# Reordering the end of a time-mixing kernel: an earlier unit's output between the last projections, and the last two slots evacuated and stored alone

## The chip, the cores and the metric

The kernel runs on one core of a Trainium2 chip. The metric is the device time of one execution in microseconds, as a median over several executions. The profile's span is shorter than that time by about 1.8 us.

## The reference

```
x_prev = x shifted by one step along the sequence, zero at the start
xv = x * time_mix_v + x_prev * (1 - time_mix_v)      # xk, k are not used by the output
xr = x * time_mix_r + x_prev * (1 - time_mix_r)
v  = xv @ value_weight;  r = xr @ receptance_weight
out = (sigmoid(r) * v) @ output_weight
```

The shapes are batch 16, sequence 2048 and width 256. Inputs and output are fp32.

## The kernel before

The work is cut into 64 units of 512 rows, four to a batch. A unit is transposed and mixed. Then come two projections (`r` and `v`, eight matmuls in all), a sigmoid on ScalarE, and a product on VectorE that gives `z`. One unit later, the output matmuls of `z` follow. The output of a unit goes from PSUM to `o_sb` by a ScalarE copy and from there to HBM by a store. Sequence rows are laid out so that a partition's row of `n` slots (a slot is 128 of the unit's rows) is one run of `n` KB in HBM.

```python
def store(queue, b, lo, hi):
    dst = out[b].rearrange("(p j) d -> p j d", p=P)
    queue.dma_start(out=dst[:, lo:hi, :], in_=o_sb[b][:, lo:hi, :])

def output(g, z):
    ...                                   # four slots of matmuls into ps (psum_o)
    nc.scalar.copy(out=o_sb[b][:, j0 : j0 + UJ, :], in_=ps)
    if b == B - 1:
        store(nc.sync, b, j0, j0 + UJ)
    elif e % 2 == 1:
        store(nc.sync, b, j0 - UJ, j0 + UJ)

def last_unit(g):                         # works by halves of 256 rows
    ...
    for h, (lo, hi) in enumerate(cols):
        project(banks[h], g, 0, lo, hi)
        nc.scalar.activation(out=s_sb[:, :, lo:hi], in_=banks[h], func=ACT.Sigmoid)
    for h, (lo, hi) in enumerate(cols):
        project(banks[2 + h], g, 1, lo, hi)
        nc.vector.tensor_tensor(out=z_sb[:, :, lo:hi], in0=s_sb[:, :, lo:hi],
                                in1=banks[2 + h], op=ALU.mult)
    ...
    for k, (pool, name) in enumerate(spare):      # k 0,1: unit before; k 2,3: this unit
        ...                                       # two slots of matmuls into ps
        if h == 0:
            nc.scalar.copy(out=o_sb[b][:, lo : lo + H, :], in_=ps)
        else:
            nc.vector.tensor_copy(out=o_sb[b][:, lo : lo + H, :], in_=ps)
        store(nc.scalar if k == 3 else nc.sync, b, lo, lo + H)
```

## Time and profile before

| what | value | read from |
|---|---|---|
| time | 213.88 us (213.71 to 214.05) | three executions |
| span | 212.8 us | the page; its execution took 214.59 us, longer than the three |
| first projection of the last unit starts | 203.70 us | the timeline |
| last copy ends | 207.43 + 0.69 = 208.12 us | the timeline |
| last store is issued / lands | 208.15 / 211.66 us | the timeline; 3.5 us to landing |
| **tail**: last unit's first projection to the end of the span | 212.83 - 203.70 = 9.13 us | worked out |

"At 3.83" in a tail means 3.83 us after the start of the last unit's first projection. The drain is the time in which the data of the stores flow out, and a landing is one of the sixteen completions that the records hold for each store. Instruction times are read from the timeline; first packets, instruction packets and landings are read from the packet and semaphore records of the same trace. Differences of such times can be off by 0.01. This is the part of it before the lines that the prediction shows. The columns are start, duration, engine, line, operation, output and inputs, shapes and count; a bracket tells the idle time before and what ended it.

```profile
203.70 0.60 PE L240 MATMUL psum_r<-mix,w_bf 128*128 128x256 bf16 x4
203.90 1.01 ACT L270 COPY o_sb<-psum_o 128x1024 f32<-128x1024 f32 x1 [0.66 <-PE psum_o L250]
...
204.93 3.25 SPq L260 DMA_DIRECT2D out_dram<-o_sb  x4
...
205.44 0.69 DVE L290 TENSOR_TENSOR z_sb<-s_sb,psum_v 128x512 bf16<-128x512 bf16 x1 [0.95 <-ACT s_sb L287]
```

ScalarE is in the copy of an earlier unit until 204.91, so its sigmoids, and with them VectorE's products, run late, and VectorE idles for 0.95 us. TensorE has work throughout, which the change uses.

### The profile page before, as it was taken

The page shows a single profiled execution, that of the slowest core. Times are in us where ns is not written, and L with a number is a line of the kernel's source. Part 1 is how long each engine was busy: PE and PEld are TensorE (multiplying, and loading weights), DVE is VectorE, ACT ScalarE, POOL GpSimd, SP SyncE. Part 2 cuts the span into 40 slices and gives each one's busy share as a digit, 9 for nine tenths or more (in the row PEclk, how much of TensorE's full clock was granted, in tenths as well). Part 3 has the DMA queues.
Part 4 walks back from the last instruction along what each step waited for, and adds up shares of the span by engine and source line. Part 5 has one row for each costly group of instructions (what it writes and reads, how often), then busy time and mean ns, then how long its engine had stood idle before and what let it go on. Part 6 is the DMA issues. An engine that isn't in the chain of part 4 may idle for free.

```text
span 212.8 us, 4177 instructions
## 1 busy us (share of the span) xinstructions
PE 202.0 (95%) x1566; PEld 134.9 (63%) x1593; DVE 193.8 (91%) x311; ACT 186.9 (88%) x202; POOL 77.1 (36%) x104
## 2 busy tenths in 40 slices
PE   8879999999999999999999999999999999999990
PEld 7537676666666666666666666666666666665570
DVE  1899999999999999999999999998999999999971
ACT  2688999998999999999999999999999999999870
POOL 1802331344453435434452444335343442344200
PEclk9999999999999999999999999999999999999998
DMA  5899999999969989998989999898989944443565
GB/s 181 196 176 216 240 288 285 326 234 337 245 152 288 277 228 339 176 348 179 291 243 225 340 200 354 157 325 211 260 283 216 354 200 197 197 172 162 208 249 200
DMA packets 9340, 51.91 MB, mean 244 GB/s; under 512 B 996, under 2 KB 1896, under 8 KB 3688
## 3 DMA queue, kind: packets, MB, share of 16 engines
q0 software_dynamic: 3008, 16.39, 43.9%
q1 hardware_dynamic: 6016, 34.87, 40.0%
q10 hardware_dynamic: 296, 0.40, 0.5%
q8 instruction: 12, 0.20, 0.3%
q14 instruction: 8, 0.07, 0.1%
HBM read 34.47 MB, written 33.55 MB: 320 GB/s over the span
## 4 chain that ended last, share of the span: by engine, by line
PE 73%; DVE 11%; DMA 5%; ACT 4%; issue 4%; POOL 1%; ACTq 0%; DVEq 0%
PE psum_o L250 22%; PE psum_v L240 20%; PE psum_r L240 19%; PE ps_t L173 10%; DVE z_sb L432 4%; DVE mix L229 3%; DMA x_bf<-in_x_dram 3%; DVE mix L207 2%; ACT s_sb L411 2%; DMA x_last<-in_x_dram 2%; ACT xt L178 1%; ACT o_sb L270 1%; PE ps_t L240 0%; ACTq L98 0%; POOL wo_bf L118 0%
## 5 line engine op out<-in xcount | busy, mean ns | idle before, releaser
L217 POOL TENSOR_SCALAR mix<-xt,c_sb 128x1024 bf16<-128x1024 bf16 (+1 forms) x61 | 64.4, 1057 | 117.0 <-DVE mix L229 101.4
L229 DVE TENSOR_TENSOR mix<-mix,xt 128x1024 bf16<-128x1024 bf16 (+1 forms) x129 | 90.0, 700 | 3.0 <-DVE mix L207 0.5
L432 DVE TENSOR_TENSOR z_sb<-s_sb,psum_v 128x1024 bf16<-128x1024 bf16 x63 | 76.6, 1216 | 4.8 <-PE psum_v L240 2.6
L270 ACT COPY o_sb<-psum_o 128x1024 f32<-128x1024 f32 x62 | 62.9, 1015 | 13.6 <-PE psum_o L250 13.2
L240 PEld LDWEIGHTS <-w_bf 128*128 128x128 bf16 x520 | 48.2, 98 | 35.4 <-issue 1.9
L240 PE MATMUL psum_v<-mix,w_bf 128*128 128x512 bf16 (+1 forms) x241 | 63.9, 377 | 1.7 <-DVE z_sb L432 0.6
L411 ACT ACTIVATE s_sb<-psum_r 128x1024 bf16<-128x1024 f32 x63 | 65.1, 1033 | 0.1
L250 PE MATMUL psum_o<-wo_bf,z_sb 128*128 128x256 bf16 x500 | 64.9, 273 | 0.2
L240 PE MATMUL psum_r<-mix,w_bf 128*128 128x512 bf16 (+1 forms) x244 | 64.0, 377 | 0.5
L178 ACT COPY xt<-ps_t 128x1024 bf16<-128x1024 bf16 x62 | 63.0, 1024 | 0.9 <-PE ps_t L173 0.9
L250 PEld LDWEIGHTS <-z_sb 128*128 128x128 bf16 x512 | 50.0, 98 | 19.1
L173 PEld LDWEIGHTS <-x_bf 128*128 128x128 bf16 x496 | 32.4, 98 | 15.6 <-DMA x_bf<-in_x_dram 2.4
L173 PE MATMUL ps_t<-ident,x_bf 128*128 128x128 bf16 x496 | 37.2, 219 | 1.6 <-DMA x_bf<-in_x_dram 1.4
L207 DVE TENSOR_SCALAR mix<-xt,c_sb 128x1024 bf16<-128x1024 bf16 (+2 forms) x89 | 35.5, 423 | 0.2
L91 POOL DMA_DIRECT2D x_bf<-in_x_dram x19 | 10.9, 577 | 0.0
L129 PE MATMUL ps_t<-zeros 128*128 128x128 bf16 x46 | 4.6, 289 | 1.0 <-DVE zeros L79 1.0
L129 PEld LDWEIGHTS <-zeros 128*128 128x128 bf16 x46 | 4.3, 135 | 1.0 <-DVE zeros L79 1.0
L399 ACT ACTIVATE mix<-xt,c_sb 128x512 bf16<-128x512 bf16 (+1 forms) x4 | 3.6, 930 | 0.0
L147 DVE COPY tm<-psum_o 128x4 f32<-128x4 f32 x1 | 0.2, 161 | 3.5 <-PE psum_o L143 3.5
L325 DVE COPY xt<-xt 128x254 bf16<-128x254 bf16 x15 | 3.3, 218 | 0.0
L112 ACT ACT_TABLE_LOAD x1 | 1.3, 1283 | 2.0 <-issue 2.0
L193 ACT CAST xt<-psum_r 128x512 bf16<-128x512 f32 x1 | 0.6, 585 | 2.5 <-PE psum_r L187 2.5
(45 smaller groups left out, 22.5 us busy)
## 6 DMA issues: line engine op xcount, KB each, us to landing
out_dram<-o_sb SPq DMA_DIRECT2D x30, 1024.0 KB, 7.1
x_bf<-in_x_dram POOLq DMA_DIRECT2D x14, 1024.0 KB, 10.8
x_bf<-in_x_dram POOLq DMA_DIRECT2D x4, 256.0 KB, 7.2
out_dram<-o_sb SPq DMA_DIRECT2D x2, 512.0 KB, 2.6
out_dram<-o_sb SPq DMA_DIRECT2D x3, 256.0 KB, 2.1
x_unit<-in_x_dram SPq DMA_DIRECT2D x2, 256.0 KB, 3.9
x_unit<-in_x_dram SPq DMA_DIRECT2D x1, 512.0 KB, 5.6
x_bf<-in_x_dram POOLq DMA_DIRECT2D x1, 512.0 KB, 10.9
```

Of the source, the lines that this page charges most:

```text
L91: nc.gpsimd.dma_start(out=x_bf[b][:, lo:hi, :], in_=rows(b)[:, lo:hi, :])
L129: nc.tensor.matmul(out=ps, lhsT=zeros, rhs=zeros, start=True, stop=True)
L173: nc.tensor.transpose(out=ps[:, ko, jj * P : (jj + 1) * P], in_=src[:, jj, ko * P : (ko + 1) * P], identity=idn,)
L178: nc.scalar.copy(out=xt[b][:, :, c0 : c0 + TU], in_=ps)
L207: nc.vector.tensor_scalar(out=mix[b][:, m, ko, lo:hi], in0=xt[b][:, ko, lo:hi], scalar1=c_sb[:, m, ko : ko + 1], scalar2=None, op0=ALU.mult,)
L217: op = nc.gpsimd.tensor_scalar(out=mix[b][:, m, 1, lo:hi], in0=xt[b][:, 1, lo:hi], scalar1=c_sb[:, m, 1:2], scalar2=1.0, op0=ALU.mult, op1 ...
L229: return nc.vector.tensor_tensor(out=mix[b][:, m, :, lo:hi], in0=mix[b][:, m, :, lo:hi], in1=xt[b][:, :, lo + P : hi + P], op=ALU.add,)
L240: nc.tensor.matmul(out=ps[:, mo, :], lhsT=w_bf[:, m, ko, mo * P : (mo + 1) * P], rhs=mix[b][:, m, ko, e * TU + lo : e * TU + hi], start=(k ...
L250: nc.tensor.matmul(out=ps[:, slot, :], lhsT=z[:, ko, jj * P : (jj + 1) * P], rhs=wo_bf[:, ko, :], start=(ko == 0), stop=(ko == KO - 1),)
L270: nc.scalar.copy(out=o_sb[b][:, j0 : j0 + UJ, :], in_=ps)
L411: nc.scalar.activation(out=s_sb, in_=ps_r, func=ACT.Sigmoid)
L432: nc.vector.tensor_tensor(out=z_sb, in0=s_sb, in1=ps_v, op=ALU.mult)
```

## The change

The intent is to start the evacuation and the stores of the last unit but one earlier, and to make the very last evacuation and store small. The first half of that unit's output moves ahead of the last value projection, and the second half follows it. ScalarE evacuates both halves, and VectorE the last unit's first half. The last two slots each get a bank (the code's word for a PSUM tile that takes one result), a copy (one on ScalarE, one on VectorE) and a store of 128 KB (one from Scalar, one from Sync). The core of the diff:

```diff
+        def out_part(pool, name, z, unit, jj, n, copy, queue):
+            ps = pool.tile([P, n, D], FP32, name=name)
+            for k in range(n):
+                out_matmuls(ps, z, jj + k, k)
+            lo = unit * UJ + jj
+            copy(out=o_sb[b][:, lo : lo + n, :], in_=ps)
+            store(queue, b, lo, lo + n)
+
+        by_act, by_dve = nc.scalar.copy, nc.vector.tensor_copy
 ...
         for h, (lo, hi) in enumerate(cols):
             project(banks[2 + h], g, 1, lo, hi)
             nc.vector.tensor_tensor(...)
-        ... (the loop over k shown above)
+            pool, name = [(ps_o_pool, "psum_o"), (ps_r_pool, "psum_r")][h]
+            out_part(pool, name, z_prev, e - 1, h * H, H, by_act, nc.sync)
+        out_part(ps_v_pool, "psum_v", z_sb, e, 0, H, by_dve, nc.sync)
+        out_part(ps_t_pool, "ps_t", z_sb, e, H, 1, by_act, nc.scalar)
+        out_part(ps_t_pool, "ps_t", z_sb, e, H + 1, 1, by_dve, nc.sync)
```

More of the change, by code (lines that the diff above doesn't have):

```diff
@@ L292, in last_unit @@
             )
-        spare = [(ps_o_pool, "psum_o"), (ps_r_pool, "psum_r"), (ps_v_pool, "psum_v"), (ps_t_pool, "ps_t")]
-        for k, (pool, name) in enumerate(spare):
-            ps = pool.tile([P, H, D], FP32, name=name)
-            h = k % 2
-            for jj in range(H):
-                out_matmuls(ps, z_prev if k < 2 else z_sb, h * H + jj, jj)
-            lo = (e - 1) * UJ + k * H
-            if h == 0:
-                nc.scalar.copy(out=o_sb[b][:, lo : lo + H, :], in_=ps)
-            else:
-                nc.vector.tensor_copy(out=o_sb[b][:, lo : lo + H, :], in_=ps)
-            store(nc.scalar if k == 3 else nc.sync, b, lo, lo + H)
+            pool, name = [(ps_o_pool, "psum_o"), (ps_r_pool, "psum_r")][h]
[3 more added lines that the diff above has]
+        out_part(ps_t_pool, "ps_t", z_sb, e, H + 1, 1, by_dve, nc.sync)
     def tile_for(b):
```

## The prediction

> **What bounds the kernel now.** I read the page's busy shares first, then its chain of waits, then only the last ten microseconds, because the diff touches nothing earlier: the instruction orders of the two kernels are the same on every engine up to the last unit.
>
> ```profile
> PE 202.0 (95%) x1566; PEld 134.9 (63%) x1593; DVE 193.8 (91%) x311; ACT 186.9 (88%) x202; POOL 77.1 (36%) x104
> PE 73%; DVE 11%; DMA 5%; ACT 4%; issue 4%; POOL 1%; ACTq 0%; DVEq 0%
> ```
>
> The body is bound by TensorE (95% busy, 73% of the chain). The change keeps the number of matmuls and only reorders the last ones, so the body's time stays. What it can move is the end: evacuations and stores after the last projections. The timeline of the last unit (start, duration, engine, line, operation; bracket: idle time before):
>
> ```profile
> 204.80 0.60 ACT L287 ACTIVATE s_sb<-psum_r 128x512 bf16<-128x512 f32 x1
> 205.29 0.60 ACT L287 ACTIVATE s_sb<-ps_t 128x512 bf16<-128x512 f32 x1
> ...
> 206.05 0.68 DVE L290 TENSOR_TENSOR z_sb<-s_sb,ps_t 128x512 bf16<-128x512 bf16 x1
> 206.08 0.59 ACT L301 COPY o_sb<-psum_o 128x512 f32<-128x512 f32 x1 [0.18 <-PE psum_o L250]
> ...
> 206.64 0.68 DVE L303 COPY o_sb<-psum_r 128x512 f32<-128x512 f32 x1
> 206.78 0.61 PE L250 MATMUL ps_t<-wo_bf,z_sb 128*128 128x256 bf16 x4
> 206.95 0.59 ACT L301 COPY o_sb<-psum_v 128x512 f32<-128x512 f32 x1 [0.29 <-PE psum_v L250]
> 207.43 0.69 DVE L303 COPY o_sb<-ps_t 128x512 f32<-128x512 f32 x1
> 208.15 0.38 ACTq L260 DMA_DIRECT2D out_dram<-o_sb  x1
> ```
>
> Computing ends at 208.12, but the span at 212.8: 4.7 us are transfers and the closing barrier. What the closing wait is for, from the waits of the Sync queue after 206 us, and the DMA view from 207 to 211.4 us (40 slices of 0.11 us):
>
> ```profile
> SPq L468 <- DMA out_dram<-o_sb: 3.3, 4, 1.4
> DMA  2000288999999999999999989989981320010000
> q1 hardware_dynamic: 450, 0.79, 48.3%
> q10 hardware_dynamic: 144, 0.26, 16.2%
> q14 instruction: 2, 0.02, 1.3%
> out_dram<-o_sb SPq DMA_DIRECT2D x3, 256.0 KB, 2.1
> out_dram<-o_sb ACTq DMA_DIRECT2D x1, 256.0 KB, 3.5
> ```
>
> The reader should see three things. The DMA engines are idle from 207.1 to 207.5, then full until 210.3: four stores of 256 KB (1.05 MB) back to back, so the drain is bound by bytes, not by the last copy. The last store lands 3.5 us after its issue, at 208.15 + 3.5 = 211.65, against 2.1 us for the stores ahead of it, since it queues. And there is a thin tail after 210.3, in which queue 14 moves two 8 KB packets of instructions: in the packet records 15 of the 16 completion packets of the last store start by 210.44, and the last one at 211.18. From the last landing to the end are 212.83 - 211.66 = 1.17 us of further waits and barrier.
>
> [...]
>
> **The change part by part.** Four matmuls of 128x256 take 0.44 us in the chain (109 ns spacing).
>
> First, the output of the earlier unit's first half moves ahead of the last value projection. Its matmuls end at 205.61 instead of 206.04. They need the psum_o bank, which ScalarE's 128x1024 copy leaves at 204.91 (203.90 + 1.01); PE gets there at 205.01, so I expect no stall, or under 0.1 us. The copy does not gain the whole 0.44: ScalarE is in the second sigmoid until 205.89, and its successive halves start 0.49 apart, so the copy starts at 205.29 + 0.49 = 205.78 and ends at 206.37, against 206.67 before. Its store goes out 0.3 us earlier, at about 206.40.
>
> Second, the last value projection ends 0.44 later, at 206.04. VectorE could start that product no earlier than 206.05 before; now at about 206.08. It loses 0.03 us, and PE's first matmul on it goes from 206.78 to 206.81. This is the main reason why the reorder costs nothing.
>
> Third, the earlier unit's second half: PE still ends it at 206.48, but ScalarE takes it (206.52 to 207.11) instead of VectorE (206.64 to 207.32). Store 0.21 us earlier, at about 207.14.
>
> Fourth, the last unit's first half moves from ScalarE (206.95 to 207.54) to VectorE (206.96 to 207.64). Before, its store had to wait for Sync, which needs 0.33 us plus 0.13 between issues, until 207.81; now it goes at 207.67. Gain 0.14.
>
> Fifth, the last two slots. With slopes from this trace (ScalarE (1012 - 586)/512 = 0.83 ns an element, VectorE (1216 - 690)/512 = 1.03) a 256-wide copy is 0.37 us on ScalarE and 0.42 on VectorE. Slot one: PE done at about 207.19, copied by 207.60, store from Scalar at 207.63. Slot two: PE done at 207.42, VectorE free to start at 206.96 + 0.60 = 207.56, done at 207.98; but Sync is issuing until 208.00 and needs 0.13 more, so it issues at 208.13. Before, the last issue was at 208.15. **So the last issue does not move**; only the bytes behind it shrink from 256 to 128 KB.
>
> What counts is then the drain. First data follow an issue by 0.8 us (206.69 to 207.5). The first store's data can start at 206.40 + 0.8 = 207.2, just as the 512 KB store ahead ends, so the idle 0.3 us is filled. The second is ready at 207.14 + 0.8 = 207.95, the first needs until 207.9: a gap of 0.05. Later ones queue. The drain took 210.44 - 207.5 = 2.94 us. The last two stores now have 1 KB packets: 46 ns median (the 1 KB loads of this trace) against 84 for the 2 KB packets of the tail, 8 packets per engine and store, so 2 x 8 x (46 - 42) = 0.06 us more. New end: 207.2 + 2.94 + 0.05 + 0.06 = 210.25 instead of 210.44, a gain of 0.19. The closing wait takes completion semaphores in a fixed order at 0.065 us each: four came after the last store's before, now three. Sum: about 0.25 us off. To this I add a little for the chance below: **213.55 us**.
>
> **The rivals.** (a) The fetch tail. In this execution instruction packets held one engine's last completion from about 210.79 (the other landings) to 211.66: 0.87 us. If the moved instructions shift or split that fetch, up to 0.87 + 0.25 = 1.1 us goes, 212.8. For: it is only two packets, and Scalar reaches its end branch at 208.0 instead of 208.5. Against: whatever its moment, the fetch still adds its time to an engine that has a full queue. I give it one in six. (b) The Sync queue becomes the bound: five issues, and if Scalar's issue at 207.63 excludes Sync's at 207.67 (both issues near 208.15 show about 0.37 instead of 0.33), the last goes at about 208.45, its data at 209.25. The queue is still full until after 210, so nothing or 0.1 us is lost: 213.7 to 213.9. (c) The drain is limited by the last copy, as the intent supposes: the gain is then the last copy's, 208.12 to 207.98, some 0.14 us: 213.7. The full DMA slices speak against it. (d) PE stalls on psum_o and pushes everything: at most 0.1 us, against a slack of 0.1 in the records.
>
> **Range and chances.** The mechanism bounds the gain at the idle hole (0.3 to 0.4 us) unless the fetch tail goes too, and the kernel before itself spreads over 213.71 to 214.05. So 212.9 to 214.1. Two per cent is 4.3 us, nearly all of the 4.7 us after the last copy; neither side is plausible: 0.01 faster, 0.98 same, 0.01 slower.
>
> **What would show it.** Right: the earlier half's copy at about 205.8, stores issued near 206.4 and 207.1, no idle DMA slice between 207.1 and 207.5, the last issue still at 208.1 or later, last packets near 210.25. Wrong: if the drain is no longer full before the last store (then the last issue decides), if 1 KB packets take far more than 46 ns, or if the two instruction packets land elsewhere or not in the tail.

## The result, and the profile after

Two sets of rounds were run. Here and in all the experiments, a ratio is the mean time of one kernel's fast runs over that of the other's of the same rounds, so it is not quite the ratio of the medians quoted.

| | median, us | before, same rounds | ratio, 95% interval |
|---|---|---|---|
| after, first | 214.00 (213.70 to 214.58) | 213.86 | 1.0009 (0.9993 to 1.0025) |
| after, again | 213.70 (213.63 to 214.22) | 213.86 | 0.9997 (0.9981 to 1.0014) |

The times do not tell the two kernels apart. The page of the changed kernel shows the same body; the chain of waits is the third line:

```profile
span 212.4 us, 4180 instructions
PE 201.5 (95%) x1566; PEld 134.6 (63%) x1593; DVE 193.8 (91%) x311; ACT 187.1 (88%) x203; POOL 77.3 (36%) x104
PE 74%; DVE 10%; DMA 5%; issue 4%; ACT 2%; POOL 1%; ACTq 0%; DVEq 0%
```

The end of its timeline:

```profile
203.56 0.60 PE L240 MATMUL psum_r<-mix,w_bf 128*128 128x256 bf16 x4
...
204.87 0.60 PE L250 MATMUL psum_o<-wo_bf,z_sb 128*128 128x256 bf16 x4
...
205.31 0.60 PE L240 MATMUL ps_t<-mix,w_bf 128*128 128x256 bf16 x4
...
205.64 0.60 ACT L291 COPY o_sb<-psum_o 128x512 f32<-128x512 f32 x1
...
206.01 0.69 DVE L300 TENSOR_TENSOR z_sb<-s_sb,ps_t 128x512 bf16<-128x512 bf16 x1
...
206.38 0.59 ACT L291 COPY o_sb<-psum_r 128x512 f32<-128x512 f32 x1
206.76 0.33 PEld L250 LDWEIGHTS <-z_sb 128*128 128x128 bf16 x4 [0.26 <-DVE z_sb L300]
...
206.82 0.69 DVE L291 COPY o_sb<-psum_v 128x512 f32<-128x512 f32 x1
207.19 0.37 ACT L291 COPY o_sb<-ps_t 128x256 f32<-128x256 f32 x1 [0.22 <-PE ps_t L250]
207.43 0.41 DVE L291 COPY o_sb<-ps_t 128x256 f32<-128x256 f32 x1
207.59 0.38 ACTq L260 DMA_DIRECT2D out_dram<-o_sb  x1
```

The reader should see that the output matmuls at 204.87 stand between the value projections, that the copies of the earlier unit are early, and that the last copy ends at 207.84. Only one matmul group pays: the first matmul on the last unit's second half waits for VectorE (0.26 us idle on the weight side). The DMA view from 207 to 211.4 us and the closing wait of the Sync queue, as shown for the kernel before:

```profile
DMA  0898998889999999999998999994210100000000
...
q14 instruction: 2, 0.02, 0.9%
...
out_dram<-o_sb SPq DMA_DIRECT2D x1, 128.0 KB, 3.3
```

```profile
SPq L471 <- DMA out_dram<-o_sb: 2.3, 3, 1.5
```

The idle hole ahead of the drain is gone (0.1 us is left of 0.4). The two instruction packets are still there, and so is the thin tail behind the data. On the common clock of the tail, in microseconds (stores named by what they carry: first and second half of the earlier unit, first half of the last unit, last two slots):

| in the tail | before | after |
|---|---|---|
| stores issued | 2.99, 3.65, 4.11, 4.45 | 2.71, 3.43, 3.98, 4.03 and 4.42 |
| first data packet | 3.83 | 3.55 |
| 8 KB instruction packets start | 6.52, 6.75 | 6.32, 6.60 |
| last landing | 7.96 | 7.76 |
| end of span | 9.13 | 8.86 |

So the tail became 0.27 us shorter: 0.20 in the last landing and about 0.07 in the waits behind it. The repetition gave 8.84 for the same kernel. Why the times do not show it is seen at the other end. From the ninth unit's first projection to the last unit's, both kernels need 166.71 us (203.70 - 36.99 and 203.56 - 36.85), and the repetition needs 166.70. But the ninth unit starts at 36.99, 36.85 and 36.31 us in these three profiles. In these profiles the starts therefore scatter by 0.7 us, more than twice the tail's gain. The other executions have no profile, so that their times differ by the start is inferred. It is not shown that this gain of the tail reaches the whole time: the first interval, 0.9993 to 1.0025, leaves out the 0.9987 that the gain alone would give.

### The profile page after: what moved, and what is told of

Its sections match the earlier page's. It is cut to its first block, busy times and chain, and to the rows that moved or that the text cites. A ratio compares the mean times of both kernels' runs of the same rounds, so it can differ in the third digit from the quotient of the medians.

```text
span 212.4 us, 4180 instructions
## 1 busy us (share of the span) xinstructions
PE 201.5 (95%) x1566; PEld 134.6 (63%) x1593; DVE 193.8 (91%) x311; ACT 187.1 (88%) x203; POOL 77.3 (36%) x104
## 4 chain that ended last, share of the span: by engine, by line
PE 74%; DVE 10%; DMA 5%; issue 4%; ACT 2%; POOL 1%; ACTq 0%; DVEq 0%
PE psum_o L250 22%; PE psum_v L240 21%; PE psum_r L240 20%; PE ps_t L173 10%; DVE z_sb L435 4%; DVE mix L229 3%; DMA x_bf<-in_x_dram 3%; DVE mix L207 2%; ACT s_sb L414 2%; DMA x_last<-in_x_dram 2%; ACT xt L178 0%; PE ps_t L240 0%; ACTq L98 0%; POOL wo_bf L118 0%; DVE o_sb L291 0%
```

## The experiments

The first four kernels ran on one chip, the next four on a second and the last four on a third, each set beside its own runs of the kernel before.

**The changed kernel again.**

> The changed kernel unaltered, to settle its time. In the two profiles the tail, from the start of the last unit's first projection to the end of the span, fell from 212.83 - 203.70 = 9.13 us to 212.42 - 203.56 = 8.86. Theory (the store drain ends earlier and nothing else changes): ratio about 0.9987, that is 0.27 us less. Rival (something outside the tail costs what the tail gains, or the tail of one profile was luck): ratio 1.000 or above, as in the first measurement (1.0009). In the profile: last landing again about 7.8 us after the start of the last unit.

Measured: 213.70 us, ratio 0.9997 (0.9981 to 1.0014), tail 8.84, last landing at 7.76. The tail's gain is real and repeats to 0.02 us. The interval includes both 0.9987 and 1.000, so this time settles nothing by itself.

**The reorder alone.**

```diff
-            out_part(pool, name, z_prev, e - 1, h * H, H, by_act, nc.sync)
-        out_part(ps_v_pool, "psum_v", z_sb, e, 0, H, by_dve, nc.sync)
-        out_part(ps_t_pool, "ps_t", z_sb, e, H, 1, by_act, nc.scalar)
-        out_part(ps_t_pool, "ps_t", z_sb, e, H + 1, 1, by_dve, nc.sync)
+            out_part(pool, name, z_prev, e - 1, h * H, H, [by_act, by_dve][h], nc.sync)
+        out_part(ps_v_pool, "psum_v", z_sb, e, 0, H, by_act, nc.sync)
+        out_part(ps_t_pool, "ps_t", z_sb, e, H, H, by_dve, nc.scalar)
```

> The reorder alone: the earlier unit's first half before the last value projection, but the evacuations on the engines of before and the last two slots together. Theory (the drain is bound by the time at which data are there and then by bytes): the first store goes out 0.3 us earlier, but the second still waits for VectorE and goes when it went before, so the hole in the DMA moves from before the first store to behind it: tail 9.05 to 9.15 us, ratio 1.000. Rival (the first store's time alone decides): tail 8.85, ratio 0.9987.

Measured: 214.38 us, ratio 1.0025 (1.0006 to 1.0043), tail 9.31. The DMA view from 206.9 to 211 us (slices of 0.10 us) shows the hole at the place expected:

```profile
DMA  5999998100399998999999999999997110101000
```

The first store starts at 3.56 and is done by 4.3; then the engines idle until the second arrives. The tail is 0.16 us worse than my range allowed. Of the 0.18 us that it is longer than before, 0.11 is in the last landing and 0.07 in the closing waits, among which the last store had an earlier place. VectorE has to finish the last product first (to 3.14 us) before it can copy the second half, so the second store goes out at 3.77, later than the 3.65 of before, and so do all stores after it (4.23 and 4.57 against 4.11 and 4.45). An early first store was worth nothing with the others later.

**The other half alone.**

```diff
-            pool, name = [(ps_o_pool, "psum_o"), (ps_r_pool, "psum_r")][h]
-            out_part(pool, name, z_prev, e - 1, h * H, H, by_act, nc.sync)
+        out_part(ps_o_pool, "psum_o", z_prev, e - 1, 0, H, by_act, nc.sync)
+        out_part(ps_r_pool, "psum_r", z_prev, e - 1, H, H, by_act, nc.sync)
```

> The other half alone: matmuls in the order of before, ScalarE evacuates both halves of the earlier unit, VectorE the last unit's first half, the last two slots each alone. Theory (bytes from the first store on): the first store goes when it went before, the queue is then full to the end, so the drain ends 0.06 us later for the 1 KB packets, less 0.065 for one closing wait: tail 9.05 to 9.2 us, ratio 1.000. Rival (the last copy and the last store's size decide): tail 8.8 to 8.9, ratio 0.9987 or less.

Measured: 214.20 us, ratio 1.0016 (0.9996 to 1.0036), tail 9.20, first data at 3.83 as before. A small last store by itself gains nothing, although its last copy ends at 4.29 instead of 4.42. In both half versions two instruction packets are in the tail (last landings at 8.07 and 8.12), as in the kernel before; they were not run again without them.

**Moving VectorE's instruction packet.** The packets of queue 14 come at places that look like fixed counts of instructions: in the changed kernel VectorE had started 70, 193, 328 and 447 instructions at four of the eight, 119 to 135 apart. That these four are VectorE's was an estimate. The edit shifts VectorE's count by 24:

```diff
     warm_up(WARM)
+    pad = consts.tile([P, 1], FP32)
+    for _ in range(24):
+        nc.vector.memset(pad, 0.0)
```

> The changed kernel with 24 one-column memsets on VectorE in its idle time at the start. In the changed kernel's records 15 of the last store's 16 completions land by 210.79 and the last at 211.32, beside two 8 KB instruction packets at 209.88 and 210.16. Theory (one of these packets is VectorE's next block, fetched when it reaches a fixed count of instructions, as its earlier packets come about 128 instructions apart): with 24 more instructions one packet moves to about 195 to 200 us, and the last landing comes 0.3 to 0.8 us earlier: tail 8.1 to 8.6 us against 8.86. Rival (both packets are set off by the jump to the closing block, or by other engines): both stay in the tail, tail 8.8 to 8.9, and the time is equal or up to 1 us more if the memsets delay the start.

Measured: 214.12 us, ratio 0.9998 (0.9975 to 1.0020), tail 8.34, last landing at 7.25. The DMA view of this kernel from 206 to 211 us, with the last store's time to landing in its final column:

```profile
q14 instruction: 1, 0.01, 0.4%
...
out_dram<-o_sb SPq DMA_DIRECT2D x1, 128.0 KB, 2.8
```

The DMA view from 196 to 199 us:

```profile
q14 instruction: 1, 0.01, 0.6%
```

One packet left the tail and came at 197.5 us. At their packets VectorE had started 447 instructions without the memsets and 451 with them. The last store lands 2.8 us after its issue instead of 3.3. The tail is 0.5 us shorter than that of the changed kernel, but the time does not show it: two of the six executions took 213.1 us, the profiled one among them, and four 214.1 to 214.4. What distinguishes them the single trace can't say, and a cost of the memsets at the start of those four is not excluded here. The versions with the late stores below carry the same memsets, and their times fall by about what their tails do.

**Moving Sync's packet too, with the change and without it.**

```diff
+        elif e % 2 == 1 and b < 3:
+            store(nc.sync, b, j0 - UJ, j0)
+            store(nc.sync, b, j0, j0 + UJ)
         elif e % 2 == 1:
```

> The changed kernel with the 24 memsets on VectorE and, in the first three batches, each 1024 KB store of Sync as two of 512 KB (12 more Sync instructions). With the memsets alone one instruction packet left the tail (it came 5.6 us before the last unit) and the tail fell from 8.86 to 8.34 us; the other still came 6.64 us into it. Theory (that one is Sync's next block, as Sync reached its 80th instruction 1.0 to 1.4 us before it in both kernels): it moves to about 195 to 200 us, 3 to 8 us before the last unit, the last landing comes with the others, tail 8.15 to 8.3 us. Rival (it belongs to the jump to the closing block or to ScalarE): it stays at 6.6 us and the tail at 8.34. The median time should be 0.5 us or more under the changed kernel's on the same start; the starts of six profiles differ by up to 0.7 us, so the ratio may still be between 0.995 and 1.000.

> The kernel of before with the same memsets and the same split stores: the change's own effect without the instruction packets is then this run against e5_both_pads. Theory (the packets delay any last store that is under way): both leave the tail, which falls from 9.13 to 8.2 to 8.45 us, and the distance to e5 is the drain's gain of 0.2 plus 0.065 for a closing wait, or less if the packets cost before more. Rival (the packets do not touch the kernel before in this way): tail 9.0 to 9.2.

Measured: with the change 214.34 us, ratio 1.0016 (0.9987 to 1.0045), tail 8.24; without it 214.40, ratio 1.0005 (0.9977 to 1.0033), tail 8.34. In both, the second packet moved to 0.37 us before the last unit and no engine's completion is late any more (last landings at 7.02 and 7.07). Sync had started 82 instructions at its packet, both in the changed kernel and in the first of these. Both packets therefore go with instruction counts, one with VectorE's (447 and 451) and one with Sync's (82 and 82). They had delayed the last landing by 0.74 us after (7.76 - 7.02) and 0.89 before (7.96 - 7.07). The tails shrank by less, 0.62 and 0.79, because the edits also move the last store to an earlier place among the closing waits, which costs 0.09 to 0.12 us. Without the packets the change is worth only 0.10 us: 0.05 in the last landing and the rest in the closing waits.

The times missed, and the trace says why. Units 4 to 8 took 14.73 us in the first of the two and 14.21 in the second, against 13.49 before. The waits of the weight loads in those units of the first:

```profile
PEld L176 <- DMA x_bf<-in_x_dram: 1.3, 1, 1.3
```

A transpose waited 1.3 us for its input. With the memsets alone those units took 13.50 us. In the kernel before, the mean DMA share in these units is 1.01, and 0.93 in units 32 to 44.

**Is the drain bound by bytes or by the last copy?** Two looks, both on the version with both packets moved. The first leaves out one store (with None as its queue, `out_part` skips it; wrong rows), the second delays the last copy.

```diff
-        out_part(ps_v_pool, "psum_v", z_sb, e, 0, H, by_dve, nc.sync)
+        out_part(ps_v_pool, "psum_v", z_sb, e, 0, H, by_dve, None)
```

> e5_both_pads without the store of the last unit's first half (256 KB); those rows of the output are wrong on purpose. Copies and all other issues stay. Theory (the drain is bound by bytes, the last issue at 4.42 us having 0.6 us to spare): the last landing comes 0.5 to 0.7 us earlier than in e5. Rival (the last copy and its issue set the end): the last landing moves by less than 0.1 us.

```diff
+        slack = consts.tile([P, H, D], FP32)
+        nc.vector.tensor_copy(out=slack, in_=x_unit[:, 0, 0:H, :])
         out_part(ps_t_pool, "ps_t", z_sb, e, H + 1, 1, by_dve, nc.sync)
```

> e5_both_pads with an idle VectorE copy of 128x512 ahead of the last copy, which delays the last copy and its store by 0.3 to 0.5 us. Theory (the queue is still full when the last store comes): the last landing moves by less than 0.1 us. Rival (the last copy sets the end): it moves by the whole delay.

Measured: without 256 KB the last landing comes at 6.28 instead of 7.02, 0.74 us earlier. The delayed version's timeline:

```profile
208.07 0.42 DVE L314 COPY slack<-x_unit 128x512 f32<-128x512 f32 x1
208.24 0.38 ACTq L263 DMA_DIRECT2D out_dram<-o_sb  x1
208.40 0.42 DVE L297 COPY o_sb<-ps_t 128x256 f32<-128x256 f32 x1
```

Its last copy starts at 4.20 in the tail instead of 3.87, and the last issue goes from 4.40 to 4.64. The last landing goes from 7.02 to 7.05. So 0.24 us of delay of the last store costs 0.03, while a store of 256 KB costs 0.74: without the packets the drain is bound by what is stored and not by the last copy. Leaving out a store takes away bytes and a store at once; that the number of stores counts too is shown below.

**The split stores later.**

```diff
-        elif e % 2 == 1 and b < 3:
+        elif e % 2 == 1 and 8 <= b < 11:
```

> e5_both_pads with the split stores in batches 8 to 10 instead of 0 to 2. In e5 the four units from 4 to 8 took 14.73 us against 13.50 with the memsets alone, so the gain of the tail was lost there. Theory (the first units are short of DMA, so extra stores there delay the loads; later ones are free): units 4 to 8 take 13.5 us again, tail 8.24 as in e5, time 0.6 us under the changed kernel on the same start: ratio to before 0.995 to 0.998. Rival (split stores cost wherever they are): units 32 to 44 take over 0.3 us longer than 36.55 us.

> The kernel of before with the memsets and the late split stores. Theory: tail 8.34 us as in e6, so nearly all of the 0.9 us that can be had in this tail is the instruction packets', not the change's: ratio 0.995 to 0.998, within 0.001 of e9. Rival (the change is worth its 0.27 us of the two first profiles): tail 8.5 or more.

Measured beside 214.16 us for the kernel before: with the change 213.14, ratio 0.9956 (0.9943 to 0.9969), tail 8.25; without it 213.53, ratio 0.9972 (0.9955 to 0.9988), tail 8.34. Units 4 to 8 took 13.66 us in the first of these, and units 32 to 44 took 36.56: the splits cost nothing measurable there. The DMA views of the two drains, with the change (from 206.4 to 210.3 us, 0.10 us a slice) and without it (from 206.6 to 210.7):

```profile
DMA  8999995999998999999898999999940000000000
...
q1 hardware_dynamic: 570, 0.91, 62.6%
q10 hardware_dynamic: 144, 0.13, 9.7%
```

```profile
DMA  7000039899999999899999999999999850000000
...
q1 hardware_dynamic: 456, 0.82, 53.4%
q10 hardware_dynamic: 144, 0.26, 16.7%
```

Neither has a line for queue 14, and neither has a thin tail: where the data end, the row falls to 0 within two or three slices (9, 4, 0 and 9, 8, 5, 0). The changed kernel's row starts earlier without a hole and takes as long again at its end. The two ratios differ by 0.0016, but their intervals overlap, and only 0.09 us of it, 0.0004, is in the tails; the two profiled executions differ otherwise in the start of the ninth unit, at 36.11 and 36.64 us.

**One last store.**

```diff
-        out_part(ps_t_pool, "ps_t", z_sb, e, H, 1, by_act, nc.scalar)
-        out_part(ps_t_pool, "ps_t", z_sb, e, H + 1, 1, by_dve, nc.sync)
+        out_part(ps_t_pool, "ps_t", z_sb, e, H, 1, by_act, None)
+        out_part(ps_t_pool, "ps_t", z_sb, e, H + 1, 1, by_dve, None)
+        store(nc.sync, b, e * UJ + H, (e + 1) * UJ)
```

> e9_late_pads, but the last two slots, still copied apart by ScalarE and VectorE, leave in one store of 256 KB from Sync (2 KB packets, no store on Scalar's queue). In e5 the last 512 KB landed in 7.02 - 5.49 = 1.53 us, in e6 in 7.07 - 5.71 = 1.36. Theory (the two 128 KB stores with 1 KB packets on two queues cost 0.15 to 0.2 us of drain): the last landing comes at 6.8 to 6.9 us into the last unit, against 7.02. Rival (the store that waits for the last copy is what counts, and it is now twice as large): last landing 7.1 or later. The tail gets one closing wait of 0.06 us more for its place in their order: 8.05 to 8.2 us.

Measured: 213.24 us, ratio 0.9950 (0.9938 to 0.9962), last landing at 6.82 against 7.03 with two stores, tail 8.08. The store is issued at 4.41 in both. So storing the two slots apart, which is one of the two aims of the change, costs 0.21 us of landing. Of that, 0.09 is data (the last packet ends at 6.47 instead of 6.56) and the rest is the time from the last packet to the last landing (0.35 instead of 0.47). With two stores, the last one's sixteen completions begin at 6.82, as the Scalar store's last one has landed at 6.81, and take 0.21 us; with one store they take 0.12 (6.70 to 6.82). Whether they wait for each other, and how much is due to packet size, the number of stores or the second queue, is not shown. Against the kernel before without packets, whose last landing is at 7.06, the reorder with one last store gains 0.24, about the 0.27 by which its first data are earlier; the split gives nearly all of that back. These are differences of tails: the times with two stores and with one, 213.14 and 213.24, do not differ clearly.

**The last store's place among the closing waits.**

```diff
-        elif e % 2 == 1 and 8 <= b < 11:
+        elif e % 2 == 1 and 6 <= b < 12:
```

> e10_one_store with twelve split stores, batches 6 to 11, instead of six, so that the last store takes the last of the eight completion semaphores that the closing waits go through in order; in e10 six waits of about 0.065 us follow the one for the last store. Theory (these waits are serial and cost what they take): from the last landing to the end 0.39 us less than in e10, tail 7.65 to 7.8 us, ratio 0.993 to 0.996: the best version. Rival (the closing barrier waits for another engine anyway): last landing to end unchanged.

Measured: 212.69 us (212.44 to 213.08) beside 214.16 (213.92 to 214.46), ratio 0.9934 (0.9921 to 0.9947), tail 7.74. From the last landing to the end it takes 0.91 us instead of 1.26: the 0.35 that six waits cost. The closing wait of Sync for stores in this kernel:

```profile
SPq L479 <- DMA out_dram<-o_sb: 1.5, 3, 0.7
```

No single wait is over 0.7 us, against 1.5 in the changed kernel. This version computes the right result and beats the kernel before of the same rounds by 0.7%, clear of the noise. That is 1.4 us, as much as its tail lost (9.13 - 7.74 = 1.39), so here the tail's gain does reach the time. The changed kernel was measured only on other chips, at 214.00 and 213.70 us. The version is the change's reorder with one last store, the two packets moved and the place chosen.

The tails side by side:

| kernel | first data | last landing | end | packets in the tail |
|---|---|---|---|---|
| before | 3.83 | 7.96 | 9.13 | 2 |
| after (repeated) | 3.55 (3.55) | 7.76 (7.76) | 8.86 (8.84) | 2 |
| reorder alone | 3.56 | 8.07 | 9.31 | 2 |
| slots alone | 3.83 | 8.12 | 9.20 | 2 |
| after, VectorE's packet moved | 3.56 | 7.25 | 8.34 | 1 |
| after, both moved late | 3.56 | 7.03 | 8.25 | 0 |
| before, both moved late | 3.83 | 7.06 | 8.34 | 0 |
| one last store | 3.56 | 6.82 | 8.08 | 0 |
| and its place | 3.56 | 6.83 | 7.74 | 0 |

## Why the prediction was right or wrong

The measured medians, 214.00 and 213.70, lie in the range, and "within 2%" was right. The step by step working can be checked in the tail, where the prediction's times less 203.70 are to be compared.

- **First and second part, the reorder.** Right. The earlier half's store was predicted at 2.70 and came at 2.71, and TensorE did not stall on psum_o. The last product was to lose 0.03 us; its start went from 2.35 to 2.45, so it lost 0.10, and TensorE waited for it. The working allowed 0.04 us from the end of the projection to VectorE's start; it took 0.10 (2.35 to 2.45). That made slot one's store 0.1 later (4.03 against 3.93); the DMA row shows no hole for it.
- **Third and fourth part.** Right: 3.44 and 3.97 predicted, 3.43 and 3.98 measured.
- **Fifth part.** Right: the last issue did not move (4.43 predicted, 4.42 measured), and the copies took 0.37 and 0.41 us against 0.37 and 0.42. That the last copy is not what counts was shown by the delayed copy and the left-out store, both without the packets.
- **The drain.** Right in kind: the hole was filled and the DMA row is full behind it. The last landing moved by 0.20 us for 0.19 predicted, but that is luck, because the sum was for data that no instruction packet holds. There 15 of the last store's 16 completion packets start by 6.60, against 6.74 before and 6.55 predicted: a gain of 0.14. Without the instruction packets the last landing moved by only 0.03 to 0.05 us (7.06 to 7.03, 7.07 to 7.02). The terms can be checked there. The data of two small stores cost 0.09 us for 0.06 predicted, with 1 KB packets of 44 to 47 ns as assumed. What the sum left out is the longer way from the last packet to the last landing, 0.12 us more. In the plain kernels the packets decide the last landing. They came 0.15 to 0.20 earlier and held it up by 0.15 less (0.74 against 0.89); together with the 0.05 that is the 0.20. Why they held it up less is open.
- **The closing wait.** Right: 1.17 to 1.10 us from the last landing to the end, for one wait less. The last experiment showed the same waits at 0.35 us for six.
- **Rival (a), the fetch tail.** It did not go away in the changed kernel, as the greater chance had it. That it holds completions was right, but two and not one (before, they land at 7.40 and 7.96, the others by 7.10), and its size was near: 0.87 us estimated in the kernel before, 0.89 by experiment. I had put it down to the jump to the closing block, which no trace had shown; the two shifts tie the packets to instruction counts, VectorE's 447 and 451 and Sync's 82 and 82.
- **Rival (b), Sync and Scalar exclude each other.** Wrong: issues at 3.98 and 4.03 overlap and take 0.33 and 0.38 us; the last Sync issue took 0.40.
- **Rival (c), the last copy decides.** Refuted: 0.03 us for a delay of 0.24. **Rival (d), a stall on psum_o.** It did not happen.
- **The point, 213.55.** The sum gave 213.6 for the same start. What failed in it is the assumption that the start is the same: in the profiles the start scatters by more than the change is worth, and six executions of each did not show the gain. What makes the first units faster or slower in one execution is left open; the profiles only show that all of it happens before the ninth unit.

## What to carry to other kernels

When only the end of a kernel is changed, measure from a fixed event near the end to the last landing, not the whole time: here the tail repeats to 0.02 us while the start scatters by 0.7. Ask of a drain whether what is stored or the last issue binds it, by leaving out a store and by delaying one; if it is what is stored, start the first and the second store early and keep the last one whole (the reorder with one last store gained 0.24 us of landing here, and cutting that store in two cost 0.21). Look at the thin tail behind the data: here one or two late completions out of sixteen were held by 8 KB instruction packets, which cost 0.74 and 0.89 us, and a few more instructions elsewhere moved these out of the way. Compare last landings and not only ends, because such edits also change the last store's place among the closing waits (here 0.06 us a place).

## Figures from these traces

- Instruction packets: in the span of either kernel there are twelve of 16 KB on queue 8 and eight of 8 KB on queue 14. The last two on queue 14 took 0.31 and 0.60 us (before) and 0.31 and 0.31 us (after). They delayed the last landing by 0.89 us (kernel before) and 0.74 us (changed kernel), and shifted one with VectorE's and one with Sync's instruction count.
- From issue to data: 0.84 us from the start of Sync's issue to the first packet (2.71 to 3.55, and 2.99 to 3.83), and 0.51 from the end of the issue, which takes 0.33.
- The price of cutting the last store in two: two stores of 128 KB on two queues landed 0.21 us later than one of 256 KB: 0.09 in the data, and 0.12 because the landing followed the last packet by 0.47 us instead of 0.35.
- The closing waits for the eight completion semaphores of the stores are taken one after another, in these traces in the same order: about 0.06 us each, 0.35 us for six, so the last store's place in that order matters.
